# An embedding gather: turning the later indices by one VectorE transpose instead of by TensorE, with GpSimd leading the section

## The chip, the cores and the metric

The kernel runs on one core of a Trainium2 chip. The metric is the device time of one execution in microseconds (us), as the median of several; the profile is one execution, and its span leaves out 1.2 to 5.5 us that the device time holds, by run and chip.

The two kernels were compared where the kernel before takes 182 us.

## The reference

```python
batch, seq_len, vocab_size, d_model = 32, 512, 50000, 512

def reference(indices, embedding_table, position_embed):
    token_embed = embedding_table[indices]
    return (token_embed + position_embed).astype(np.float32)
```

Per index, one row of 2 KB is read from the table, the row of its position is added, and 2 KB are written: 33.55 MB in, 33.55 MB out.

## The kernel before

Partition `p` holds the positions `4p` to `4p+3`, so each sequence is four gathers (`k` = 0 to 3) of 128 rows. Each gather here takes one index per partition. For the first four sequences these come straight from a load. For the other 28 one large load brings the indices in with sequences on partitions, and they have to be turned so that positions lie on partitions:

```python
# ScalarE's queue: loads
nc.scalar.dma_start(out=idx0[:, 0, :], ...)            # first sequence
load_pos(0)                                            # positions, first half
nc.scalar.dma_start(out=idx0[:, 1:, :], ...)           # sequences 1 to 3
nc.scalar.dma_start(out=idx_raw[:], ...)               # all, for turning
nc.scalar.wait_ge(s_pos[0], 16)
load_pos(1)

# GpSimd: identity for TensorE, then 128 gathers
nc.gpsimd.affine_select(out=ident[:], ...).then_inc(s_prep, 1)
nc.gpsimd.wait_ge(s_first, 16)
for g, (b, k) in enumerate(order):
    if g == half:      nc.gpsimd.wait_ge(s_next, 16)
    if g == FIRST * K: nc.gpsimd.wait_ge(s_prep, 2 + K + J)   # turned indices
    # ... cut: wait for a free slot at b == SLOTS
    ins = nc.gpsimd.indirect_dma_start(out=slots[b % SLOTS][:, k, :],
        in_=table, in_offset=..., ).then_inc(s_gather[g % LANES], 16)
    if g >= LANES:
        ins._wait_ge(s_gather[g % LANES], rounds(g - LANES))

# TensorE: four transposes
nc.tensor.wait_ge(s_prep, 2)
for k in range(K):
    nc.tensor.transpose(turned[:, k]..., idx_f[:, :, k], ident[:]).then_inc(s_prep, 1)

# VectorE: adds, with the turning between them
for g, (b, k) in enumerate(order):
    if g == 7:   nc.vector.tensor_copy(out=idx_f..., in_=idx_raw[:, :, 0])  # to f32
    if g == 9:   # four casts from PSUM back to int32, one per 32 partitions
        for j in range(J):
            nc.vector.tensor_copy(out=idx_t[j*Q:(j+1)*Q], in_=turned[:, :, :, j])
    # ... cut: copies of the positions to PSUM
    nc.vector.tensor_tensor(out=part, in0=part, in1=pos_ps[:, k, :], op=add
        )._wait_ge(s_gather[g % LANES], rounds(g)).then_inc(s_add, 1)

# ScalarE's queue: stores, two rows per partition, each after its adds
```

All of this is one section of hand-set waits, led by VectorE. In the trace the leader's queue gives a marker at 0.83 us (L101); ScalarE's first load, at 1.03, and GpSimd's affine select, at 1.18, follow it. At the end the same queue has waits of this line until 173.4 us. After the section, ScalarE waits for the last stores.

## Time and profile before

| | |
|---|---|
| device time | 181.99 us, median of 3; 182.02 of 6 with those beside the comparison |
| span of the profile | 178.1 us |
| GpSimd, 128 gathers | 121.3 us busy, gap 0.305 us ahead of each but the first |
| VectorE, 128 adds | 87.7 us busy |
| moved | 68.34 MB, 384 GB/s over the span |

The first part of the page gives busy time, share of the span and number of instructions of each engine:

```profile
PE 1.0 (1%) x4; PEld 0.4 (0%) x4; DVE 91.4 (51%) x137; POOL 121.8 (68%) x133
```

No engine is near 100%. That says nothing yet: the gap of 0.305 us between two gathers is not counted as busy and, put down as "issue" (38.7 us in all), is not a wait for anything that the profile shows either.

### The profile page before, as it was taken

Reading aid. Unit: us, or ns where it says so; the run is one execution under the profiler, and the core shown is the slowest. Engines: PE = TensorE matmul, PEld = TensorE weight load, DVE = VectorE, ACT = ScalarE, POOL = GpSimd, SP = SyncE. Lnnn points to the kernel's source line nnn. Section 1 sums busy time; section 2 is a strip of 40 time slices with the busy share of each in tenths; the row PEclk is TensorE's granted clock in tenths of the full one; section 3 lists DMA queues with packets and bytes.
Section 4 is the critical chain, followed back from the end, with each engine's and each line's share of the span. In section 5 each row is a group of like instructions: output and inputs, shape, how many; then the busy total and the mean of one; then the engine's idle time right before and its main releaser. Section 6 shows DMA issues by size and latency. Waiting matters only on the chain.

```text
span 178.1 us, 415 instructions
## 1 busy us (share of the span) xinstructions
PE 1.0 (1%) x4; PEld 0.4 (0%) x4; DVE 91.4 (51%) x137; POOL 121.8 (68%) x133
## 2 busy tenths in 40 slices
PE   0000100000000000000000000000000000000000
PEld 0000000000000000000000000000000000000000
DVE  0445973455556555555556455555556555554510
POOL 3777777777777777777777777777777777774000
DMA  4899999999999999999999999999999999999960
GB/s 122 234 329 359 375 378 364 385 410 413 416 416 419 419 419 420 419 420 419 419 420 420 419 419 418 419 418 419 420 419 420 418 420 420 420 419 421 417 258 0
DMA packets 21011, 68.34 MB, mean 384 GB/s; under 512 B 3728, under 2 KB 3856, under 8 KB 21008
## 3 DMA queue, kind: packets, MB, share of 16 engines
q10 hardware_dynamic: 10768, 34.76, 48.6%
q0 software_dynamic: 10240, 33.56, 48.1%
q14 instruction: 3, 0.02, 0.0%
HBM read 34.75 MB, written 33.55 MB: 384 GB/s over the span
## 4 chain that ended last, share of the span: by engine, by line
POOL 65%; issue 23%; DMA 5%; DVE 2%; ACTq 0%; DVEq 0%
POOL slot L136 65%; DMA slot<-in_embedding_table_dram,idx_t 4%; DVE slot L171 2%; DMA idx<-in_indices_dram 1%; ACTq L211 0%; DVEq L101 0%
## 5 line engine op out<-in xcount | busy, mean ns | idle before, releaser
L136 POOL DMA_INDIRECT slot<-in_embedding_table_dram,idx_t x112 | 106.0, 946 | 34.1 <-issue 34.1
L171 DVE TENSOR_TENSOR slot<-slot,pos_ps 128x512 f32<-128x512 f32 x128 | 87.7, 687 | 73.8 <-issue 57.8
L136 POOL DMA_INDIRECT slot<-in_embedding_table_dram,idx x16 | 15.3, 958 | 6.0 <-issue 4.6
L166 DVE COPY pos_ps<-pos_sb 128x512 f32<-128x512 f32 x4 | 2.7, 685 | 4.9 <-DMA pos_sb<-in_position_embed_dram 4.9
L162 DVE CAST idx_t<-turned 32x128 int32<-32x128 f32 x4 | 1.1, 280 | 0.1
L149 PE MATMUL turned<-ident,idx_f 128*32 128x128 f32 x4 | 1.0, 413 | 17.6 <-issue 17.6
L118 POOL TENSOR_SCALAR_AFFINE_SELECT ident<-const-float32-1.0 128x128 f32<-128x128 f32 x1 | 0.3, 282 | 0.7 <-DVEq L101 0.7
L149 PEld LDWEIGHTS turned<-ident,idx_f 128*32 128x32 f32 x4 | 0.4, 131 | 17.7 <-issue 17.6
L200 POOL MEMSET const-float32-0.0<- 128x1 f32 x1 | 0.1, 99 | 0.3 <-issue 0.3
L156 DVE CAST idx_f<-idx_raw 128x128 f32<-128x128 int32 x1 | 0.2, 220 | 0.0
L200 POOL MEMSET const-uint8-127<- 128x1 uint8 x1 | 0.1, 116 | 0.0
L200 POOL MEMSET const-bfloat16-1.0<- 128x1 bf16 x1 | 0.1, 110 | 0.0
L200 POOL MEMSET const-float32-1.0<- 128x1 f32 x1 | 0.1, 102 | 0.0
## 6 DMA issues: line engine op xcount, KB each, us to landing
out_dram<-slot ACTq DMA_DIRECT2D x60, 512.0 KB
out_dram<-slot ACTq DMA_DIRECT2D x8, 256.0 KB
slot<-in_embedding_table_dram,idx_t POOLq DMA_INDIRECT x112
pos_sb<-in_position_embed_dram ACTq DMA_DIRECT2D x2, 512.0 KB, 4.7
slot<-in_embedding_table_dram,idx POOLq DMA_INDIRECT x16
idx_raw<-in_indices_dram ACTq DMA_DIRECT2D x1, 128.0 KB
idx<-in_indices_dram ACTq DMA_DIRECT2D x1, 4.0 KB, 1.6
idx<-in_indices_dram ACTq DMA_DIRECT2D x1, 12.0 KB
```

The source lines that it names most:

```text
L118: nc.gpsimd.affine_select(out=ident[:], in_=nc.const_aps.tensor(1.0, [P, P], f32), pattern=[[-1, P]], compare_op=mybir.AluOpType.is_equal, ...
L136: ins = nc.gpsimd.indirect_dma_start(out=slots[b % SLOTS][:, k, :], out_offset=None, in_=table, in_offset=bass.IndirectOffsetOnAxis(ap=whe ...
L149: nc.tensor.transpose(turned[:, k].rearrange("p b j -> p (b j)"), idx_f[:, :, k], ident[:]).then_inc(s_prep, 1)
L156: nc.vector.tensor_copy(out=idx_f[:].rearrange("r p k -> r (p k)"), in_=idx_raw[:, :, 0])._wait_ge(s_raw, 16).then_inc(s_prep, 1)
L162: nc.vector.tensor_copy(out=idx_t[j * Q : (j + 1) * Q, :, :], in_=turned[:, :, :, j]).then_inc(s_prep, 1)
L166: nc.vector.tensor_copy(out=pos_ps[:, k, :], in_=pos_sb[:, k, :])._wait_ge(s_pos[k // half], 16).then_inc(s_ps, 1)
L171: nc.vector.tensor_tensor(out=part, in0=part, in1=pos_ps[:, k, :], op=add)._wait_ge(s_gather[g % LANES], rounds(g)).then_inc(s_add, 1)
L200: nc = _bacc.Bacc("TRN2", target_bir_lowering=False, num_devices=1)
```

## The change

The intent is to drop the round trip over TensorE. Indices are read as 32-bit words (the low half of each 64-bit index), and one transpose on VectorE turns them as int32 (STREAM_TRANSPOSE, 128x128): no cast to float, no identity matrix, no PSUM, no casts back. The kernel turns them in squares of 32 and has for that the raw indices laid out with quarter `j` of every sequence on partitions `32j` to `32j+31`, so one load becomes four here. And GpSimd leads the section.

```diff
-    idx_raw = sbuf("idx_raw", [P, Q * K, 2], i32)
-    ident = sbuf("ident", [P, P], f32)
-    idx_f = sbuf("idx_f", [P, Q, K], f32)
+    idx_raw = sbuf("idx_raw", [P, 2 * Q * K], i32)
-    turned = psum("turned", [Q, K, B, J], f32)
...
-    with tc.tile_critical(sync_engine=nc.vector.engine, no_gpsimd_drain=True):
+    with tc.tile_critical(sync_engine=nc.gpsimd.engine, no_gpsimd_drain=True):
...
-        nc.scalar.dma_start(
-            out=idx_raw[:], in_=idx_rows.rearrange("r (s w) -> r s w", w=2)
-        ).then_inc(s_raw, 16)
+        for j in range(J):
+            nc.scalar.dma_start(
+                out=idx_raw[j * B : (j + 1) * B, :], in_=idx_rows[:, j, :]
+            ).then_inc(s_raw, 16)
...
-        nc.gpsimd.affine_select(... out=ident[:] ...)
...
             if g == FIRST * K:
-                nc.gpsimd.wait_ge(s_prep, 2 + K + J)
+                nc.gpsimd.wait_ge(s_idx, 1)
...
-        nc.tensor.wait_ge(s_prep, 2)
-        for k in range(K):
-            nc.tensor.transpose(...)
...
             if g == 7:
-                nc.vector.tensor_copy(out=idx_f..., in_=idx_raw[:, :, 0])
-            if g == 9:
-                ... four nc.vector.tensor_copy(out=idx_t[...], in_=turned[...])
+                nc.vector.transpose(
+                    out=idx_t[:],
+                    in_=idx_raw[:].rearrange("r (q k w) -> r k q w", k=K, w=2)[:, :, :, 0],
+                )._wait_ge(s_raw, 16 * J).then_inc(s_idx, 1)
```

More of the change, by code (lines that the diff above doesn't have):

```diff
@@ L38 @@
     assert S == P * K and B == 32
-    assert V < (1 << 24), "an index passes through float32"
     J = P // Q
+    assert B == Q, "indices are turned in squares of 32"
     idx_words = indices.bitcast(i32)
     idx_first = idx_words[0:FIRST].rearrange("b (p w) -> p b w", p=P)
-    idx_rows = idx_words.rearrange("b (j w) -> (b j) w", j=J)
+    idx_rows = idx_words.rearrange("b (j w) -> b j w", j=J)
     out_rows = out.rearrange("b (p k) d -> b p k d", k=K)
@@ L88 @@
     s_out, s_rest = sem("s_out"), sem("s_rest")
-    s_prep, s_ps, s_add = sem("s_prep"), sem("s_ps"), sem("s_add")
+    s_idx, s_ps, s_add = sem("s_idx"), sem("s_ps"), sem("s_add")
     def rounds(g):
@@ L110 @@
         )
-        nc.scalar.dma_start(
-            out=idx_raw[:], in_=idx_rows.rearrange("r (s w) -> r s w", w=2)
-        ).then_inc(s_raw, 16)
+        for j in range(J):
+            nc.scalar.dma_start(
+                out=idx_raw[j * B : (j + 1) * B, :], in_=idx_rows[:, j, :]
+            ).then_inc(s_raw, 16)
         nc.scalar.wait_ge(s_pos[0], 16)
         load_pos(1)
-        nc.gpsimd.affine_select(
-            out=ident[:], in_=nc.const_aps.tensor(1.0, [P, P], f32),
-            pattern=[[-1, P]], compare_op=mybir.AluOpType.is_equal, fill=0.0,
-            base=0, channel_multiplier=1,
-        ).then_inc(s_prep, 1)
         nc.gpsimd.wait_ge(s_first, 16)
@@ L144 @@
         nc.gpsimd.drain()
-        nc.tensor.wait_ge(s_prep, 2)
-        for k in range(K):
-            nc.tensor.transpose(
-                turned[:, k].rearrange("p b j -> p (b j)"), idx_f[:, :, k], ident[:]
-            ).then_inc(s_prep, 1)
         for g, (b, k) in enumerate(order):
             if g == 7:
-                nc.vector.tensor_copy(
-                    out=idx_f[:].rearrange("r p k -> r (p k)"), in_=idx_raw[:, :, 0]
-                )._wait_ge(s_raw, 16).then_inc(s_prep, 1)
-            if g == 9:
-                nc.vector.wait_ge(s_prep, 2 + K)
-                for j in range(J):
-                    nc.vector.tensor_copy(
-                        out=idx_t[j * Q : (j + 1) * Q, :, :], in_=turned[:, :, :, j]
-                    ).then_inc(s_prep, 1)
+                nc.vector.transpose(
+                    out=idx_t[:],
+                    in_=idx_raw[:].rearrange("r (q k w) -> r k q w", k=K, w=2)[
+                        :, :, :, 0
+                    ],
+                )._wait_ge(s_raw, 16 * J).then_inc(s_idx, 1)
             if b == 0:
```

## The prediction

The sum on the path came to -0.08 us, all of it part 2's estimate (from the marker at 0.83 us and GpSimd's last start-up event, which ends at 0.70); parts 1 and 3 to 5 stand at 0. The 0.3 us for the transpose in part 5 is the author's estimate; what is left of its grounds is the cast of the same 128x128 elements, 220 ns, and the 17.6, 5.4, 1.0 and 90.4 that follow from it are estimates too. And the size of rival (d), with the 2% given to a slowdown, was not shown: the trace has for it only a first gather of 1.14 us against 0.95 and, against it, that the affine select goes with two MODIFY_POOL_CONFIG of 11 ns each. In rivals (b) and (e) the landing of the four loads near 6 us and the "some tenths" are estimates (in the kernel before, the first index load landed 1.58 us after its issue, and the queue was to be through with the four by about 4.3 us).

> **What bounds the kernel now.** I read the page's busy shares first, then the costliest groups, the chain that ended last, the windows and the timeline of the start.
>
> The page's groups (columns: line, engine, operation, tiles, count; busy us and mean ns; idle before and what ended it):
>
> ```profile
> L136 POOL DMA_INDIRECT slot<-in_embedding_table_dram,idx_t x112 | 106.0, 946 | 34.1 <-issue 34.1
> L171 DVE TENSOR_TENSOR slot<-slot,pos_ps 128x512 f32<-128x512 f32 x128 | 87.7, 687 | 73.8 <-issue 57.8
> ...
> L162 DVE CAST idx_t<-turned 32x128 int32<-32x128 f32 x4 | 1.1, 280 | 0.1
> L149 PE MATMUL turned<-ident,idx_f 128*32 128x128 f32 x4 | 1.0, 413 | 17.6 <-issue 17.6
> L118 POOL TENSOR_SCALAR_AFFINE_SELECT ident<-const-float32-1.0 128x128 f32<-128x128 f32 x1 | 0.3, 282 | 0.7 <-DVEq L101 0.7
> ...
> L156 DVE CAST idx_f<-idx_raw 128x128 f32<-128x128 int32 x1 | 0.2, 220 | 0.0
> ```
>
> GpSimd issues 128 gathers of 128 rows by 2 KB (256 KB each), 946 ns apiece, and what stands before nearly every one is "issue": time in which it waited for nothing that the profile shows. Every other engine waits for much of the span: VectorE is idle 73.8 us ahead of its adds. All that the change removes (affine select, cast, four matmuls, four casts) is in the small rows: 0.28 + 0.22 + 1.0 + 1.1 us.
>
> The timeline of the start (start us, length us, engine, line, operation, tiles; idle before):
>
> ```profile
> 1.03 0.38 ACTq L104 DMA_DIRECT2D idx<-in_indices_dram  x1
> 1.18 0.28 POOL L118 TENSOR_SCALAR_AFFINE_SELECT ident<-const-float32-1.0 128x128 f32<-128x128 f32 x1 [0.67 <-DVEq L101]
> ...
> 2.41 0.51 ACTq L111 DMA_DIRECT2D idx_raw<-in_indices_dram  x1
> 2.89 1.14 POOL L136 DMA_INDIRECT slot<-in_embedding_table_dram,idx  x1 [1.43 <-DMA idx<-in_indices_dram]
> 4.33 0.95 POOL L136 DMA_INDIRECT slot<-in_embedding_table_dram,idx  x1 [0.31 <-issue]
> ...
> 17.30 0.22 DVE L156 CAST idx_f<-idx_raw 128x128 f32<-128x128 int32 x1
> ...
> 17.83 0.69 DVE L171 TENSOR_TENSOR slot<-slot,pos_ps 128x512 f32<-128x512 f32 x1 [0.31 <-issue]
> ...
> 19.86 1.21 DVE L162 CAST idx_t<-turned 32x128 int32<-32x128 f32 x4
> ...
> 23.09 0.95 POOL L136 DMA_INDIRECT slot<-in_embedding_table_dram,idx_t  x1 [0.30 <-issue]
> ```
>
> Three things are to be seen. The affine select ends at 1.46, and GpSimd then idles 1.43 us more until the first index load lands. From the second gather on, the gap is 0.30 us at every gather; the same timeline has the last one at 161.94, so the pace is (161.94 - 4.33) / 126 = 1.251 us, which is 0.946 + 0.305. And the seventeenth gather, the first to use the turned indices, starts at 23.09 after the same 0.30: the turned indices were complete at 19.86 + 1.21 = 21.07, 2.0 us before, so this wait costs nothing today.
>
> Is the pace GpSimd's or the DMA's? The windows (PE, PEld, DVE, POOL busy us, then clock, DMA share, GB/s):
>
> ```profile
> 40.00:100.00 60.00, 0.00 (x0) 0.00 (x0) 33.04 (x49) 45.38 (x49) 1.00 1.03 418
> 100.00:150.00 50.00, 0.00 (x0) 0.00 (x0) 27.28 (x41) 37.81 (x41) 1.00 1.03 419
> ```
>
> The DMA engines are fully busy too. But 256 KB in and 256 KB out every 1.251 us is 524,288 / 1.251 = 419 GB/s, just what is moved, and the gap of 0.30 is the same at 4 us, when the queues are nearly empty, as at 160 us. From the end of a gather's issue to its add takes about 5 us at the start and 7.0 us at 43 us, at 103 us and at 153 us: the backlog neither grows nor shrinks. GpSimd therefore sets the pace, and the DMA keeps up with nothing visible to spare.
>
> The chain that ended last at its end (start us, us, what): one gather's landing, the last adds, then the tail.
>
> ```profile
> 156.94 7.85 DMA slot<-in_embedding_table_dram,idx_t
> ...
> 169.59 0.69 DVE slot L171
> ```
>
> So the span is a sum: first gather 2.89, its 1.44 to the second, 126 x 1.251 = 157.6, the last gather's 0.94, 6.7 to its add, 0.69 for the add, 7.8 from there to the end: 2.89 + 1.44 + 157.6 + 0.94 + 6.7 + 0.69 + 7.8 = 178.1. The measured median, 181.99, lies 3.9 above the span.
>
> [...]
>
> **The change part by part.**
>
> 1. Affine select gone (0.28 us of GpSimd). It stood in a wait of 1.43 us beyond its end: worth 0 on the path.
> 2. GpSimd leads the section. Before, ScalarE's first index load waits for a marker of VectorE's queue: the chain has "0.83 0.03 DVEq L101", then the load at 1.03. GpSimd is the engine whose queue releases the start-up barrier (its event ends near 0.70), so its marker can come about 0.05 to 0.1 us sooner than one that must first see the release. I estimate 0.08 us earlier for index load, first gather and, as the pace is fixed, everything after. In the order of instructions after the change, GpSimd also has the section's closing waits; these run while ScalarE waits for its last store to land, so I give them 0.
> 3. One load of the raw indices becomes four of 32 partitions. Bytes (128 KB) and 1 KB rows are the same. ScalarE's queue issues three more, at 0.45 to 0.51 each by its neighbours: about 1.4 us, from 2.92 to about 4.3. The next issue, the second half of the positions, waits until 4.93 anyway. Worth 0; the small loads ahead of it keep their place.
> 4. TensorE part gone: four matmuls at 17.58, their wait, and the four casts. VectorE loses 0.22 + 1.1 = 1.3 us.
> 5. One VectorE transpose added, at the place of the old cast. For 128 partitions by 128 elements the cast took 220 ns[...]; I estimate 0.3 us. It starts near 17.3 and ends near 17.6, before the add at 17.83, which waits for its gather. The indices are then ready 5.4 us ahead of the seventeenth gather, rather than 2.0. As that gather was not waiting, worth 0. VectorE's net relief is 1.0 us, on an engine with 73.8 us of idle.
>
> Sum on the path: -0.08 us of 182, 0.04%. Span 178.0, time 181.9.
>
> **The rivals.**
>
> (a) The turned indices were a hidden brake, and the pace rises from the seventeenth gather on. Against it: the gap before that gather is the 0.30 of all the others. The most I could give this is 0.3 us.
>
> (b) The transpose is much slower than estimated, or waits for the four loads. For: no row of this trace has one, and its input is strided. Were it 1.3 us, the add at 17.83 would slip to about 18.6, still with gathers arriving every 1.25 and 0.69 per add, so VectorE catches up. It would have to take over 5 us to touch the seventeenth gather. Four loads on an early, busy queue may land near 6 us, far ahead of 17.3. Time unchanged.
>
> (c) The DMA is the real bound, and the earlier start only lengthens the backlog. Then the 0.08 is lost and the time is 182.0; the prediction hardly changes. Nothing in this change removes bytes.
>
> (d) Start-up of GpSimd gets dearer: without the affine select, the first gather has to pay some first use. For: the first gather takes 1.14 against 0.95 even now. [...] Against: the change removes a configuration of GpSimd and adds none.
>
> (e) Leading costs GpSimd at the end: the closing handshake comes after the last store rather than beside it. Some tenths of a microsecond, 182.3.
>
> **Range and chances.** The centre is 181.9. The runs before spread over 181.74 to 182.42, which is larger than any effect above except (d). I take 181.3 (rival a plus a good chip) to 182.5 (rival e plus spread). Faster by 2% needs 3.6 us; the whole of the work removed on all engines is 2.6 us and lies beside the path: 1%. Slower by 2% needs (d): 2%. The rest, 97%, is within 2%.
>
> **What would show each step right or wrong.** In the profile after: 128 gathers at 946 ns and a 0.30 gap, the first near 2.8, the last near 161.9; the gap before the seventeenth still 0.30; no TensorE row; one transpose row of 0.2 to 0.5 us near 17.3; VectorE's busy total down from 91.4 to about 90.4; windows at 419 GB/s; adds 7 us after their gathers. Wrong would be: a gap ahead of a gather other than the first that isn't 0.30, a first gather at 4 or later, a pace other than 1.251, or a tail after the last add that isn't 7.8.

## More of the kernel before

The experiments came in three calls, each on a chip of its own, with runs of the kernel before on that chip: 182.03 us on the first, 176.19 on the second, 181.82 on the third. Times are compared within a call only.

## The result, and the profile after

The changed kernel takes 182.48 us (182.32 to 182.52, 6 runs) against 182.02 (181.74 to 182.42, 6 runs). The ratio is 1.0021, with a 95% interval of 1.0008 to 1.0033. Ratios here are the mean time of one kernel's runs over that of the other's of the same rounds, so not quite the ratio of the medians. The 0.2% are small but clear of zero. The outputs are right.

The costliest groups of the kernel after, from its page:

```profile
L127 POOL DMA_INDIRECT slot<-in_embedding_table_dram,idx_t x112 | 106.2, 948 | 34.1 <-issue 34.1
...
L140 DVE STREAM_TRANSPOSE idx_t<-idx_raw 128x128 int32<-128x128 int32 x1 | 0.4, 399 | 0.0
```

The rows of the affine select, the matmuls and the five casts are gone, and one transpose of 399 ns has come. The gathers' row is what it was, but for 2 ns: over 126 gathers that is 0.26 us, and the last gather does start at 162.15 instead of 161.94. The timeline of its start:

```profile
0.90 0.38 ACTq L99 DMA_DIRECT2D idx<-in_indices_dram  x1
...
2.28 1.92 ACTq L107 DMA_DIRECT2D idx_raw<-in_indices_dram  x4
2.89 1.08 POOL L127 DMA_INDIRECT slot<-in_embedding_table_dram,idx  x1 [2.44 <-DMA idx<-in_indices_dram]
...
16.08 0.40 DVE L140 STREAM_TRANSPOSE idx_t<-idx_raw 128x128 int32<-128x128 int32 x1
...
18.32 0.69 DVE L152 TENSOR_TENSOR slot<-slot,pos_ps 128x512 f32<-128x512 f32 x1 [1.84 <-DMA slot<-in_embedding_table_dram,idx]
...
23.08 0.94 POOL L127 DMA_INDIRECT slot<-in_embedding_table_dram,idx_t  x1 [0.30 <-issue]
```

GpSimd's wait for the first index has grown from 1.43 to 2.44 us, because the affine select (0.28 us), and the 0.67 us of idle time ahead of it, now count as one wait with the rest: the first gather starts at 2.89 in both. The turned indices are ready at 16.48, 6.6 us ahead of the seventeenth gather, which starts at 23.08 after the same 0.30 as before (23.09 there). The work saved in front of it bought only more slack. (How much there was differs by run: with the old way of turning, 2.0 us in the kernel before and 0.8 in b_lead below, both enough.)

The windows of the kernel after (here DVE and POOL only, then clock, DMA share, GB/s) show the same steady state:

```profile
40.00:100.00 60.00, 32.84 (x48) 45.37 (x49) 1.00 1.03 415
100.00:150.00 50.00, 27.43 (x41) 37.80 (x41) 1.00 1.03 418
```

The end deserves its own view, because the two profiled runs differ by 0.23 us in device time (182.29 and 182.52), and yet the last add ends at 170.28 and 170.31. The closing instructions of the program, by queue (count, shortest/median/longest in ns, start of the first and of the last in us), in the kernel before:

```profile
L211 SPq EVENT_SEMAPHORE  x4: 28/696/1955, 169.7 to 177.4; - x4
...
L211 SPq DRAIN  x3: 7/7/700, 173.6 to 176.0; - x3
L211 ACTq COMPARE_BRANCH  x2: 33/36/38, 0.9 to 173.4; - x2
...
L211 DVEq EVENT_SEMAPHORE  x2: 21/21/21, 173.8 to 174.4; - x2
```

and in the kernel after:

```profile
L192 SPq EVENT_SEMAPHORE  x4: 17/376/703, 170.9 to 177.5; - x4
...
L192 SPq DRAIN  x3: 7/702/1397, 171.0 to 176.1; - x3
L192 ACTq COMPARE_BRANCH  x2: 33/36/38, 0.7 to 173.4; - x2
...
L192 DVEq EVENT_SEMAPHORE  x2: 21/21/21, 173.7 to 174.2; - x2
```

The last start in ScalarE's row (ACTq COMPARE_BRANCH, 173.4 in both) is read here as the moment at which it has seen the last store land. The DMA fits it: in the stretch from 172 to 173 us it still moved 264 GB/s in the kernel before and 139 in the one after, and from 173 to 174 nothing in either. So the work ends at the same time in both kernels. VectorE's last closing instruction starts at 174.4 and 174.2. SyncE (SPq), which does no work here, goes on until 178.1 and 178.2, with single instructions of 0.7 us and more. So about half of the 7.8 us that the prediction put after the last add are neither adds nor stores, but SyncE closing the program.

### The profile page after: what moved, and what is told of

Read it like the earlier page. It is cut to its first block, busy times and chain, and to the rows that moved or that the text cites. A ratio compares the mean times of both kernels' runs of the same rounds, so it can differ in the third digit from the quotient of the medians.

```text
span 178.2 us, 399 instructions
## 1 busy us (share of the span) xinstructions
DVE 90.7 (51%) x133; POOL 121.7 (68%) x132
## 2 busy tenths in 40 slices
DMA packets 21059, 68.34 MB, mean 383 GB/s; under 512 B 3776, under 2 KB 3904, under 8 KB 21056
## 3 DMA queue, kind: packets, MB, share of 16 engines
q0 software_dynamic: 10240, 33.56, 48.6%
## 4 chain that ended last, share of the span: by engine, by line
POOL 66%; issue 23%; DMA 5%; DVE 1%; POOLq 1%; ACTq 0%
POOL slot L127 66%; DMA slot<-in_embedding_table_dram,idx_t 4%; DVE slot L152 1%; DMA idx<-in_indices_dram 1%; POOLq L135 1%; ACTq L192 0%; POOLq L97 0%; POOLq L119 0%; POOLq L181 0%
```

## The experiments

In both kernels ScalarE's closing wait stands after the section and compares with a register. All experiments were made on a common base instead, with that wait inside the section and against a constant:

```diff
+        nc.scalar.wait_ge(s_rest, 16 * rest)
     tc.no_sync_barrier()
-    nc.scalar.wait_ge(s_rest, nc.scalar.to_reg(16 * rest))
```

Theory: GpSimd's pace of 1.251 us per gather sets the time, all that the change removes lies beside it, and the 0.4 us come from elsewhere. The rivals were that the DMA is the bound and GpSimd only fills its backlog, that part of GpSimd's pace is back-pressure, and, for the 0.4 us, the new leader, the four loads, the missing work, or the closing.

### First chip: the change in its two halves

**b_const**: the kernel before on the base.

> The kernel before with one edit: ScalarE's closing wait for the last stores stands inside the section, against a constant. It is the base of the next three. Both theories: pace 1.251 us, gathers 946 ns, first gather at 2.89; the section's closing handshake now follows the landing of the last store instead of running beside it, so 0 to 0.4 us longer than before, 182.0 to 182.4.

Measured: 182.22 us, ratio to the kernel before 1.0014 (0.9997 to 1.0031). The base costs nothing that can be told from zero, though its interval leaves room for 0.3%. (The first gather started at 3.03, not at the 2.89 written ahead: its index load took 1.73 us instead of 1.58.)

**b_lead**: the leader alone.

```diff
-    with tc.tile_critical(sync_engine=nc.vector.engine, no_gpsimd_drain=True):
+    with tc.tile_critical(sync_engine=nc.gpsimd.engine, no_gpsimd_drain=True):
```

> That base, with GpSimd leading the section in place of VectorE, nothing else. Theory A (the 0.4 us that the change cost come from no part of the work removed or added, but from 2 ns more per gather, which follow the leading engine or the run): if it is the leader, gathers take 948 ns here and the time is 0.2 to 0.5 us above the base. Theory B (the 0.4 us come with the turning of the indices, four loads and the buffers that fell away): gathers at 946 ns and the time within 0.1 us of the base.

Measured: 182.07 us, ratio 1.0014 (0.9994 to 1.0033), gathers at 946 ns. The leader neither costs nor gains. In the two profiles the marker stands at 0.76 instead of 0.83 us and the first index load is issued at 0.96 instead of 1.03, so the marker does come 0.07 us sooner. From issue to landing that load takes 1.62 us here, 1.73 in b_const, 1.58 in the kernel before and 1.72 in the one after: a spread larger than the gain.

**a_vec**: the other half alone, the whole change with VectorE still leading (the same edit the other way round).

> The same base with the other half of the change alone: four loads, the VectorE transpose, no affine select, no TensorE, VectorE still leading. Theory B: 948 ns per gather, 0.2 to 0.5 us above the base. Theory A: 946 ns and within 0.1 us of the base.

Measured: 182.56 us, ratio 1.0030 (1.0015 to 1.0045), but gathers at 946 ns and a pace of 1.250. The time is as theory B had it; the mechanism it named, slower gathers, is absent.

**a_const**: the whole change on the base.

> The whole change on that base. Both theories: about 0.4 us above the base, since the change measured 182.48 against 182.02. If it is at the base instead, the 0.4 us were not in the change's work at all but in the closing waits that this base alters, or in the spread between chips.

Measured: 182.48 us, ratio 1.0029 (1.0015 to 1.0044), gathers at 946 ns; 0.26 us above the base by the medians, where 0.4 was written ahead. Over the twelve runs of each, the two kernels with the turning half lie 0.31 us above the two without (mean 182.53 against 182.22, standard error of the difference 0.09). So the excess belongs to the turning half, and not to the leader. It isn't in GpSimd's pace, as the 946 ns show. In this profile ScalarE passed its closing wait at 172.6 us, 1.6 us *earlier* than in b_const's (174.3), and yet the device times of these two profiled runs are 182.40 and 182.22. All four profiles of this call agree: the last instruction of any engine but SyncE ends at 175.5 (b_const) and 174.9 (b_lead) without the turning half, and at 174.5 (a_vec) and 173.8 (a_const) with it, so the slower kernels are done sooner. In this call, then, the device time does not follow the end of the work within 1.7 us (175.5 against 173.8, at 182.22 against 182.40).

### Second chip: is the pace GpSimd's?

On this chip the kernel before takes 176.19 us. **a_late** takes the whole change and moves the transpose so late that the seventeenth gather must wait:

```diff
-            if g == 7:
+            if g == 14:
                 nc.vector.transpose(
```

> The whole change on the common base, with the transpose moved from the seventh add to the fourteenth, so that the seventeenth gather has to wait for it. In the profile after the change the fourteenth add ends near 25.7, so that gather should start near 26.3 in place of 23.1: 3.2 us of stall. Theory (GpSimd's pace sets the time, a lost slot is never made up): pace 1.251 before and after it, last gather near 165.1, adds 6.5 to 7 us after their gathers again by the end, time 182.5 + 3.2 = 185.7. Rival (the DMA is the bound and GpSimd only fills its backlog): the stall is paid from the backlog, the delay from gather to add falls by about 3 us for good, time within 0.5 of 182.5.

Measured: 180.36 us (179.54 to 181.93), ratio 1.0253 (1.0207 to 1.0298): 4.2 us above the kernel before by the medians (the 185.7 written ahead was for a chip of 182 us, so 3.2 above). The timeline of this kernel at the stall, and its last gather:

```profile
25.48 0.40 DVE L140 STREAM_TRANSPOSE idx_t<-idx_raw 128x128 int32<-128x128 int32 x1
...
26.66 0.94 POOL L127 DMA_INDIRECT slot<-in_embedding_table_dram,idx_t  x1 [4.03 <-DVE idx_t L140]
...
165.43 0.95 POOL L127 DMA_INDIRECT slot<-in_embedding_table_dram,idx_t  x1 [0.30 <-issue]
```

The stall is 4.03 - 0.30 = 3.7 us, more than the 3.2 expected, as GpSimd starts 0.8 us after the transpose ends. The last gather starts at 165.43, against 161.68 and 161.78 in a_1load and a_dead of the same call (below): all 3.7 us are still there 111 gathers later, and the 4.2 us agree with them within the interval (3.6 to 5.3 us). The delay from a gather's end to its add, taken here as the measure of the bytes asked for and not yet moved (from issue to landing this run's later gathers took 7.0 us, median, against 0.95 us for the instruction), fell to 3.7 us just after the stall, and was 6.2 again halfway and 6.9 at the end. The slot that GpSimd lost was not made up: the rival as it was worded, with the stall paid from the backlog for good and a time within 0.5 us, falls. How much room the DMA has is another matter. After the stall it never went above 421 GB/s in a slice of the page, and no slice of any run here is above 425. No run issues gathers faster, so how soon the DMA would be the next limit is not shown. This is also what a wait for the turned indices *would* have cost, had there been one.

**a_half** stores half the columns, so its result is wrong:

```diff
-                out=out_rows[b][:, at : at + n, :],
-                in_=slots[b % SLOTS][:, at : at + n, :],
+                out=out_rows[b][:, at : at + n, : D // 2],
+                in_=slots[b % SLOTS][:, at : at + n, : D // 2],
```

> The whole change on the common base, stores of the first 256 of 512 columns only, so a wrong result on purpose: 16.8 MB of 68.3 fewer to move, GpSimd's work untouched. Theory: 946 ns, gap 0.305, pace 1.251 as before, last gather near 161.9; only the delay from gather to add falls, from 6.5 to perhaps 3, and the time by 3 to 4 us to about 179. Rival (part of the 946 or of the 0.305 is back-pressure of full DMA queues): the pace falls below 1.2 and the time below 172.

Measured: 172.68 us, ratio 0.9806 (0.9769 to 0.9842), 3.5 us less than the kernel before by the medians (at 2% the verdict is "unclear", as the interval includes 0.98; clear of zero it is). The expected 179 was for a chip of 182 us; the gain was the 3 to 4 us named. Gathers at 945 ns, gap 0.305, last gather at 161.64; the last add comes 4.2 us after its gather. With a quarter of the bytes gone, and the delay from gather to add down to 4 to 5.5 us in the steady part (about 6 to 8 in the kernels that move all bytes), the pace does not move at all, so neither the 946 ns nor the gap is back-pressure. Here the bytes count only through the last backlog (in the kernel after, 6.5 us from the last gather to its add). (The edit takes away bytes, not packets: there are 28,739 in all against 21,059, and the 7,680 more are 128 for each of the 60 larger stores.) Its gathers, a window, and the queue of its gather packets (packets, MB, share of 16 engines' span):

```profile
L127 POOL DMA_INDIRECT slot<-in_embedding_table_dram,idx_t x112 | 105.9, 945 | 34.1 <-issue 34.1
```

```profile
40.00:100.00 60.00, 32.39 (x48) 45.38 (x49) 1.00 0.97 313
```

```profile
q0 software_dynamic: 10240, 33.56, 62.6%
```

Against 415 to 419 GB/s at a share of 1.03, this kernel moves 313 at a share of 0.97. In the kernel after, the same 10,240 gather packets of the same 33.56 MB are put down with 48.6% of the engines' span: 87 us of 178.2, against 107 us of 170.6 here. So the recorded time of the same packets differs by a quarter with what else is moved, and a share of 1.03, above the whole stretch, holds times that overlap. A share near 1, as the 0.97 at 313 GB/s here, does not by itself show that the DMA engines are at their limit.

**a_1load**: one load for the four, in the new order.

```diff
-        for j in range(J):
-            nc.scalar.dma_start(
-                out=idx_raw[j * B : (j + 1) * B, :], in_=idx_rows[:, j, :]
-            ).then_inc(s_raw, 16)
+        nc.scalar.dma_start(
+            out=idx_raw[:], in_=idx_rows.rearrange("b j w -> j b w")
+        ).then_inc(s_raw, 16)
...
-                )._wait_ge(s_raw, 16 * J).then_inc(s_idx, 1)
+                )._wait_ge(s_raw, 16).then_inc(s_idx, 1)
```

> The whole change on the common base, with the four loads of raw indices as one load of 128 partitions in the new order. If the three extra loads carry the 0.3 us by which the kernels with the turning part lie above those without (182.5 against 182.2), the time is 182.2; if not, 182.5. Pace 1.251 either way.

**a_dead**: affine select and TensorE transposes put back as dead work.

```diff
+        nc.gpsimd.affine_select(out=ident[:], ...).then_inc(s_prep, 1)
         nc.gpsimd.wait_ge(s_first, 16)
...
+        nc.tensor.wait_ge(s_prep, 1)
+        for k in range(K):
+            nc.tensor.transpose(turned[:], ident[:], ident[:]).then_inc(s_prep, 1)
```

> The whole change on the common base, with an affine select on GpSimd and four TensorE transposes of its output put back as dead work that nobody waits for. If the 0.3 us come from what is missing (an idle TensorE, a GpSimd without its configuration and affine select, the place of the buffers), the time is 182.2; if it comes from the four loads or the transpose, 182.5. Pace 1.251 either way; the affine select again ends inside the wait for the first index.

Measured: 176.20 us, ratio 0.9988 (0.9962 to 1.0014), and 176.13 us, ratio 0.9991 (0.9964 to 1.0018). Both are level with the kernel before, but the absolute times written ahead were for a chip of 182 us, and without the plain change or the bare base on this chip the two could not be judged as meant. What they do show is the closing. In a_dead:

```profile
L204 SPq EVENT_SEMAPHORE  x4: 17/40/2600, 170.3 to 173.9; - x4
...
L204 SPq DRAIN  x3: 7/7/7, 173.1 to 173.4; - x3
...
L204 DVEq EVENT_SEMAPHORE  x2: 21/21/21, 173.3 to 173.9; - x2
```

Here SyncE's last instruction starts with VectorE's, at 173.9, and its drains take 7 ns instead of up to 1,397. (Its 2,600 ns entry starts at 170.3 and lasts until 172.9.) That accounts for the 6 us between the chips: in the four profiles of this call the device time is 1.7 to 1.8 us above the end of the last instruction of any engine but SyncE, in those of the other two calls 6.7 to 8.6.

### Third chip: the excess again, and an attempt at a faster version

**a_const2**: the whole change on the base, as in a_const.

> The whole change on the common base again, for a second chip: the last call ran on one where the kernel before takes 176.2 in place of 182.0, with SyncE's queue closing beside the others rather than 4 us after them. Theory (the 0.3 to 0.4 us that the change costs lie in the slow closing of SyncE's queue, not in the work): on a chip with the short closing, within 0.1% of the kernel before; on one with the long closing, 0.2 to 0.3% above it again. Rival (they lie in the work): 0.2 to 0.3% above on every chip.

**a_1load2**: as a_1load.

> As the last one, with one load for the four. If the extra loads carry the 0.3 us, below that one by 0.3 us; if not, level with it within 0.15 us.

**a_dead2**: as a_dead.

> As the first, with the affine select and TensorE transposes put back as dead work. If what is missing carries the 0.3 us (TensorE's place in the section's closing, say), below the first by 0.3 us; if not, level with it within 0.15 us.

Measured: 182.17, 182.12 and 182.15 us against 181.82, ratios 1.0018 (1.0002 to 1.0034), 1.0018 (1.0002 to 1.0035) and 1.0020 (1.0004 to 1.0036). This chip closes slowly again: in a_const2 SyncE goes on until 179.9, the others end at 174.7. And 0.3 us above the kernel before are back, equal in all three, so neither the four loads nor the missing work carries them. How much of them is the turning half is not shown here: the bare base was not run on this chip, and on the first it stood at 1.0014 (0.9997 to 1.0031) itself. In a_1load2 the gathers took 948 ns, in a_1load, the same kernel, 946: those 2 ns, which the profile after also shows, go with the run and not with the change.

**a_store4**: larger stores, as an attempt at a version faster than both.

```diff
+        elif b >= FIRST:
+            if k == K - 1:
+                stores.append((g + 1, b, 0, K))
         elif k % half == half - 1:
             stores.append((g + 1, b, k + 1 - half, half))
```

> An attempt at a faster version: from the fifth sequence on, one store of all four rows per partition (8 KB) in place of two of 4 KB, and so 26 stores fewer. GpSimd's pace is untouched at 1.251, so by the theory the only gain is a shorter backlog: if larger stores cost the DMA engines less, the delay from gather to add falls from 6.5 towards the 4.2 of the run with half the store bytes, and the time by 1 to 2 us. If packets cost the same whatever the store, 0; the later release of each store could then cost up to 1 us.

Measured: 182.28 us, ratio 1.0023 (1.0006 to 1.0039), against 182.17 for a_const2: no gain. The last add comes 6.1 us after its gather instead of 7.0, but the last gather itself started at 162.18 instead of 161.93. No kernel here with a right result beats the kernel before.

## Why the prediction was right or wrong

The prediction (181.9 us, 181.3 to 182.5) held: 182.48, only just inside the upper end, and two of the six runs lie above it. Its main argument held because each part removed stood beside a fixed pace. The 0.6 us above the centre have a source that it did not name, and that they fitted into a range drawn for rival (e) was luck.

- *GpSimd sets the pace.* Right, and now shown from both sides: a stall of 3.7 us stays in full (a_late), and a quarter fewer bytes leave the pace where it is (a_half). Rival (c) falls with these, and so does any back-pressure in the pace. The added phrase that the DMA keeps up "with nothing visible to spare" leaned in part on a share of 1.03, which a_half shows to be a poor gauge; whether there is room to spare stays open. (Its "about 5 us at the start" is 2.6 us for the first gather and 4.6 for the sixth. Its "nearly empty" queues at 4 us are not a measured depth: one gather and four loads had been issued by then, and the DMA moved 222 GB/s from 4 to 8 us, against 418 and 419 later.)
- *Parts 1 and 4, affine select and TensorE part, worth 0.* Right: first gather at 2.89 in both, gap before the seventeenth 0.30 in both; putting dead work back changes nothing (a_dead2 against a_const2).
- *Part 2, the leader, -0.08 us.* That GpSimd's queue is first out of the start-up is in the trace: its last event there ends at 0.702 us, those of the other four queues start at 0.726 to 0.738. The marker came 0.07 us sooner (b_lead), but the index load's own spread of 0.15 us is larger, and no time followed: 182.07 against 182.22, within the noise. In the profile after, the load was issued 0.13 us sooner and took 0.14 longer.
- *Part 3, four loads, worth 0.* Right: ScalarE's queue was through with them at 4.20, ahead of its next issue, and one load is no faster (a_1load2 against a_const2).
- *Part 5, the transpose, 0.3 us.* It took 0.40 (399 ns; 398 and 399 in a_half and a_late), and ended at 16.48. It cost nothing there: the following add waited until 18.32 for its gather. VectorE's total fell from 91.4 to 90.7, not to 90.4: 1.3 removed, 0.4 added, and 0.2 more in the adds.
- *Rivals.* (a) and (b) fall by the gap of 0.30. (d) did not happen: the first gather took 1.08 us, against 1.14 before. (e) fell as worded: GpSimd's lead costs nothing (b_lead).

What was off is the last tenths: -0.08 us predicted, and 0.46 more by the medians, 0.2% by the ratio. The step that failed is the term "7.8 from there to the end", which the prediction took as the tail of the last stores and as fixed. Some 3.6 us of it are SyncE's closing (others done at 174.4, span 178.1), and that term differs by chip and by run: it is 7.9 in the kernel after, 9.4 in a_vec, and 4.2 in a_1load on the chip with the short closing. Where the profiles show the closing go on after all other engines, it does so for 3.6 us (kernel before) to 5.2 (a_const2); on the second chip it does not at all (a_late, a_dead). The excess comes with the turning half (0.31 us, first chip). It is not in the leader or in the gathers' pace and, as far as it is present on the third chip, not in the four loads or the missing work. The last store was seen to land at 173.4 in both profiles, so in these two runs the excess lies after the work. On the chip with the short closing, two variants of the change were level with the kernel before. All this points to SyncE's closing. It is not shown, for three reasons: the intervals on that chip reach to 1.0014 and 1.0018, neither the plain change nor the bare base ran there, and no run altered that closing alone. Why the turning half should lengthen it stays open.

## What to carry to other kernels

Before shortening a preparation, look at the gap ahead of its first user: where it equals all the other gaps, as the 0.30 us here, the preparation is hidden, and taking it away buys slack alone (6.6 us of it here in place of 2.0). To find which of two busy resources sets a pace, stall one on purpose and take bytes off the other; a stall that is never made up (3.7 us here), together with a pace that the missing bytes leave as it is (945 ns and 0.305 us with a quarter gone), names the bound. And before explaining tenths of a microsecond, look at where the work ends and what the program still does after it.
